# Low halves of q in zero-padded tiles of 128 rows for the score products of a hybrid decoder trunk

## The chip, the cores and the metric

The kernel runs on one core of a Trainium2 chip. The metric is the device time of one execution in microseconds. The engines are named PE (TensorE, the matrix products), DVE (VectorE), ACT (ScalarE), POOL (GpSimd) and SP (SyncE, which issues DMAs here). PEld is PE's weight load: a product on PE holds one operand (lhsT) in its array and streams the other (rhs) past it.

## The reference, cut to what matters

Two layers, each a half-step feed-forward network, a token mixer with four branches (A short convolution, B long convolution, C differential attention, D forgetting attention), and another feed-forward network. T = 512 tokens, model width 1024, fp32. The change touches the scores of C and D:

```python
# C: 4 heads x 2 maps of 64 channels, values of 128 channels
logits = jnp.einsum('bqhmd,bkhmd->bmhqk', q[:, q0:q1], k[:, :q1]) * scale + bias   # bias: -slope * distance
p = jax.nn.softmax(logits, axis=-1)
pd = p[:, 0] - lam * p[:, 1]
outs.append(jnp.einsum('bhqk,bkhd->bqhd', pd, v[:, :q1]))
...
# D: 8 heads of 64 channels
logits = jnp.einsum('bqhd,bkhd->bhqk', q[:, q0:q1], k[:, :q1]) * scale + bias      # bias: cumulative log forget gate, causal
p = jax.nn.softmax(logits, axis=-1)
outs.append(jnp.einsum('bhqk,bkhd->bqhd', p, v[:, :q1]))
```

Queries go in blocks of 128, so block i sees the keys 0 to 128 (i + 1).

## The kernel before

**Exact halves.** Every fp32 operand is a sum of a rounded high half and a low half, both in a format that PE multiplies at full rate (F32R). A product of two operands is made of high x high, high x low and low x high. For the projections and the feed-forward networks `mm3` (L127 to L131) issues the three: L129 is w_hi x_hi, L130 w_hi x_lo, L131 w_lo x_hi, with weight blocks of 128x128 as lhsT and 512 columns of x as rhs. The weights stream from memory in chunks of 8 blocks; `load` issues the DMA on SP, ACT casts the high half (L99), DVE subtracts the low half (L100).

**Queries and keys.** `q_of` and `k_of` each run one projection of 24 products for two maps of 64 channels: map 0 in partitions 0 to 63, map 1 in 64 to 127 (the slices `LANES`). `q_of` scales q by -1/8 on DVE (L476); ACT writes each map's high halves to both halves of the partitions of a tile of its own (`qh`, two tiles), and DVE writes the low halves of both maps into one tile `ql`, each map in its own 64 partitions. `k_of` puts the high halves of a map in its own 64 partitions and the low halves in the other 64. A score then takes two products: L501 with all 128 rows (q_hi against k_hi and against k_lo at once), and L502 with the 64 rows of the map's lanes (q_lo against k_hi):

```python
PE.matmul(out=p[:, :n], lhsT=q[0][m][:, c], rhs=k[m][:, :n], start=True, stop=False)
PE.matmul(out=p[:, :n], lhsT=q[1][r, c], rhs=k[m][r, :n], start=False, stop=not masked)
```

The columns n are 256, 256, 384 and 512 for the query blocks 0 to 3 (at least 256). In D a third product in bf16 (L504, 128 columns) adds the causal mask; in C the mask lies in the bias tile.

**What follows a score.** DVE adds the bias and takes the row's extreme (L519), ACT takes the exponential with its sum (L521). In C, `combine` (L597 to L600) forms p0 - lambda p1 of a row block on DVE; in D, `scale_rows` divides by the sum (L704, L705). `transposed` (L531) turns the row blocks by ten 128x128 transposes on PE, ACT and DVE make high and low halves of them (`ph` L150, `pl` L143), and `weigh` (L547) multiplies by the values.

**The order of work.** PE takes its products in the order in which the code emits them. For one C head that is: scores of query blocks 0 and 1 (eight products of 256 columns), the q projection of the next head, scores of blocks 2 and 3 (four of 384 and four of 512), the k projection, the output products of branch A (`merge`, 12), the ten transposes, a gate projection, weigh, another merge, sums over partitions, a gate, and the spread of a row of norms (L187). For one of the eight sets of D (a pair of heads x 2 maps) it is: the scores of four blocks with their masks, the q or k projection of the next pair (for the last pair a gate), the transposes, a gate, weigh, a merge. DVE's and ACT's work is set by the same code: `late` holds low halves and other second steps, which `settle` issues behind the next group of products, and `spare` holds the taps of B's long convolution (L383), which `cover` takes one at a time behind groups in C. In C, DVE keeps the order of the code (`manual_schedule`). The combination of the last row block (`combine(NQ - 1)`) is queued in `late` and comes behind the products of the k projection.

**Places.** Work tiles of 128x512 take places from the pool `sp` (65 of them), taken over by a new tile when the old one's last reader is done. Permanent tiles lie in the pool `cp`. PSUM has 8 places.

Of the kernel before, what the change touches and what calls it, by code (L numbers as in the profile page):

```python
# [15 lines left out]
P = 128  # L16
# [10 lines left out]
# column offsets of w_in  # L27
# [9 lines left out]
# chunks of weights that are loaded and split ahead of their use  # L37
AHEAD = 3
# taps of the long convolution that go with a group of products: in A and B, in C, in D
PACE = (3, 1, 5)  # L40
# steps of a boundary's second half in front of the first half's sums and of its spread norms
# [14 lines left out]
def build(tc, ws, xT, vecs, wdf, lamv, fb, consts, outT):  # L56
    """Emits the program; returns the order in which it takes the 128 x 128 blocks of the weights from ws."""
    nc = tc.nc
    order = []
    with ExitStack() as ctx:  # L60
        cp = ctx.enter_context(tc.tile_pool(name="cp", bufs=1))
        sp = ctx.enter_context(tc.tile_pool(name="sp", bufs=65))
# [22 lines left out]
        # the stream of weight blocks  # L85
# [4 lines left out]
        def load(c, parts=1):  # L90
            """the hi and lo halves of chunk c of the stream"""
# [23 lines left out]
        # work that later groups of products are to cover  # L115
# [11 lines left out]
        def mm3(out, w, x, first, last):  # L127
            """out += w.T @ x with both operands in exact halves."""
            PE.matmul(out=out, lhsT=w[0], rhs=x[0], start=first, stop=False)  # L129
            PE.matmul(out=out, lhsT=w[0], rhs=x[1], start=False, stop=False)  # L130
            PE.matmul(out=out, lhsT=w[1], rhs=x[0], start=False, stop=last)  # L131
# [22 lines left out]
        def split(src, scale=None, s="x"):  # L154
            """hi and lo halves of a tile, optionally times a scale first; the lo halves come with the next group."""
# [5 lines left out]
        def colsum(col, acc, c):  # L161
            """per-token sums over the partitions of acc[:, c], as columns."""
# [4 lines left out]
        def rstd(col, width, factor=1.0):  # L167
            """factor * (sums / width + eps) ** -0.5"""
# [7 lines left out]
        def diagonals(r):  # L176
            """a per-token column set on the diagonals of squares"""
# [6 lines left out]
        def spread(out, dg, n):  # L184
            """the diagonals of n squares as a row, the same in all partitions."""
# [4 lines left out]
        def rows_of(acc, width):  # L190
            """rstd of the sums over acc's partitions; the diagonals come with the next group."""
# [7 lines left out]
        def square_into(acc, src):  # L199
            """acc + src ** 2; acc None: src ** 2"""  # L200
# [7 lines left out]
        def boundary(post, pre, first):  # L208
            """h += factor * rms_norm(y) * g with y = products of post, then g * h of the next stage in halves,
            its first six groups of products and the per-token rstd as columns and as rows.  # L210

            The last tile of y and the first groups go by halves of the tokens, so that one half's norms are
            covered by the other half's products."""
            xs = []

            def new_x(k, c):
                """hi now, lo as a closure"""
# [8 lines left out]
            def outer(k, c):  # L226
                """products of row block k for the first four groups and the tokens c"""
# [17 lines left out]
            else:  # L245
# [10 lines left out]
                def last(a, b, h):  # L256
                    """steps a to b of the trailing tiles' products for the token half h"""
# [78 lines left out]
        # ---- feed-forward  # L336
# [29 lines left out]
        # ---- token mixing  # L366
# [6 lines left out]
        def mixer(l, entry):  # L373
# [13 lines left out]
            # lambda, on all partitions  # L387
# [15 lines left out]
            # B: gated linear unit and long convolution  # L403
# [22 lines left out]
            # A: short convolution  # L426
# [16 lines left out]
            def values(c0):  # L443
                """by tokens: [token, 512 channels] for each block of 128 tokens"""
# [15 lines left out]
            def paired(p, scale):  # L460
                """64-channel heads' halves side by side, for 128 output partitions: [hi lo] of even, [lo hi] of odd"""
# [11 lines left out]
            def q_of(c0):  # L473
                """-q/8 of two 64-channel maps: each map's hi halves on both halves of the partitions; lo halves"""
                q = slot()
                V.scalar_tensor_tensor(out=q, in0=proj(c0), scalar=-0.125, in1=rb, op0=ALU.mult, op1=ALU.mult)  # L476
                hi, lo = [slot(F32R, "qh"), slot(F32R, "qh")], slot(F32R, "ql")
# [4 lines left out]
                late.extend(lambda m=m: lo_of(lo[LANES[m]], q[LANES[m]], hi[m][LANES[m]]) for m in range(2))  # L482
# [348 lines left out]
```

## Time and profile before

| what | value |
|---|---|
| median of 3 runs | 2768.29 us (2768.15 to 2768.41) |
| span of the profiled execution, first to last instruction | 2767.0 us |
| mean granted TensorE clock | 0.998 |
| PE busy | 2748.0 us, 99% of the span, 13196 instructions |
| PEld busy | 2288.5 us, 83% |
| DVE busy | 1617.2 us, 58% |
| ACT busy | 1014.9 us, 37% |
| POOL busy | 57.0 us, 2% |
| HBM read, over the span | 250.48 MB, 91 GB/s |

The profiled execution has no time of its own beside its span; the span is 1.3 us under the median of the runs. Products on PE are pipelined, so the durations of neighbouring products overlap, and the distance from one start to the next tells how long PE needs for one. PEld rows are weight loads; a load that lies under the product before it costs nothing. The share of busy time is an average over stages. Which wait ends last in the attention stages is read from the timeline of these stages.

### The profile page before, as it was taken

Reading aid. Unit: us, or ns where it says so; the run is one execution under the profiler, and the core shown is the slowest. Engines: PE = TensorE matmul, PEld = TensorE weight load, DVE = VectorE, ACT = ScalarE, POOL = GpSimd, SP = SyncE. Lnnn points to the kernel's source line nnn. Section 1 sums busy time; section 2 is a strip of 40 time slices with the busy share of each in tenths; the row PEclk is TensorE's granted clock in tenths of the full one; section 3 lists DMA queues with packets and bytes.
Section 4 is the critical chain, followed back from the end, with each engine's and each line's share of the span. In section 5 each row is a group of like instructions: output and inputs, shape, how many; then the busy total and the mean of one; then the engine's idle time right before and its main releaser. Section 6 shows DMA issues by size and latency. Waiting matters only on the chain.

```text
span 2767.0 us, 33140 instructions
## 1 busy us (share of the span) xinstructions
PE 2748.0 (99%) x13196; PEld 2288.5 (83%) x13196; DVE 1617.2 (58%) x2699; ACT 1014.9 (37%) x1569; POOL 57.0 (2%) x84
## 2 busy tenths in 40 slices
PE   9999999999999999999999999999999999999998
PEld 7888898878778898888888888988777788988887
DVE  6444269878686555442364432798777765554423
ACT  4322242444553343332342222424445533433221
POOL 0000000001000000000000000000010000000000
PEclk9999999999999999999999999999999999999999
DMA  4332222222222223233233322232222223222331
GB/s 169 99 99 95 96 94 93 84 69 77 88 77 96 92 84 106 92 99 99 84 99 99 97 94 99 86 99 78 68 84 84 81 88 99 92 95 96 99 99 54
DMA packets 73787, 254.75 MB, mean 92 GB/s; under 512 B 8465, under 2 KB 10897, under 8 KB 73633
## 3 DMA queue, kind: packets, MB, share of 16 engines
q1 hardware_dynamic: 69264, 246.45, 27.4%
q10 hardware_dynamic: 4368, 6.20, 0.8%
q8 instruction: 103, 1.69, 0.2%
q14 instruction: 52, 0.42, 0.1%
HBM read 250.48 MB, written 2.13 MB: 91 GB/s over the span
## 4 chain that ended last, share of the span: by engine, by line
PE 99%; DVE 0%; DMA 0%; ACT 0%; POOLq 0%; issue 0%; DVEq 0%; ACTq 0%
PE p L129 27%; PE p L131 27%; PE p L130 27%; PE pf L130 2%; PE pf L129 2%; PE pf L131 2%; PE sc L502 2%; PE o L547 1%; PE pl L129 1%; PE pl L131 1%; PE pl L130 1%; PE sc L501 1%; PE pv L454 1%; PE pv L453 1%; PE pv L455 1%; PE pt L531 1%
## 5 line engine op out<-in xcount | busy, mean ns | idle before, releaser
L99 ACT CAST wh<-raw 128x1024 fp32r<-128x1024 f32 (+1 forms) x465 | 488.4, 1051 | 1303.5 <-PE p L130 865.4
L129 PE MATMUL p<-xh,wh 128*128 128x512 f32 x2304 | 904.9, 393 | 0.0
L131 PE MATMUL p<-xh,wl 128*128 128x512 f32 x2304 | 897.4, 389 | 0.0
L130 PE MATMUL p<-xl,wh 128*128 128x512 f32 x2304 | 897.0, 389 | 0.0
L100 DVE TENSOR_TENSOR wl<-raw,wh 128x1024 fp32r<-128x1024 f32 (+1 forms) x465 | 566.7, 1219 | 396.2 <-ACT wh L99 395.3
L129 PEld LDWEIGHTS p<-xh,wh 128*128 128x128 f32 x2304 | 432.8, 188 | 90.8 <-issue 2.0
L131 PEld LDWEIGHTS p<-xh,wl 128*128 128x128 f32 x2304 | 432.4, 188 | 91.0
L130 PEld LDWEIGHTS p<-xl,wh 128*128 128x128 f32 x2304 | 432.7, 188 | 88.3 <-issue 0.5
L129 PE MATMUL p<-gh,wh 128*128 128x512 f32 x616 | 239.6, 389 | 0.0
L130 PE MATMUL p<-gl,wh 128*128 128x512 f32 x616 | 239.6, 389 | 0.0
L131 PE MATMUL p<-gh,wl 128*128 128x512 f32 x616 | 239.6, 389 | 0.0
L352 DVE TENSOR_TENSOR s<-p,rb 128x512 f32<-128x512 f32 x80 | 55.2, 691 | 238.8 <-PE p L131 238.8
L383 DVE SCALAR_TENSOR_TENSOR yc<-ba,vec,yc 128x489 f32<-128x489 f32 (+18 forms) x240 | 171.6, 728 | 1.8
L346 DVE TENSOR_TENSOR s<-p,rb 128x512 f32<-128x512 f32 x80 | 55.2, 690 | 153.4 <-PE p L131 153.3
L129 PEld LDWEIGHTS p<-gh,wh 128*128 128x128 f32 x616 | 115.6, 188 | 24.1
L130 PEld LDWEIGHTS p<-gl,wh 128*128 128x128 f32 x616 | 115.6, 188 | 24.1
L131 PEld LDWEIGHTS p<-gh,wl 128*128 128x128 f32 x616 | 115.6, 188 | 23.9
L129 PE MATMUL pf<-xh,wh 128*128 128x256 f32 (+1 forms) x352 | 104.5, 297 | 6.9 <-ACT wh L99 6.9
L130 PE MATMUL pf<-xl,wh 128*128 128x256 f32 (+1 forms) x352 | 104.4, 297 | 0.0
L131 PE MATMUL pf<-xh,wl 128*128 128x256 f32 (+1 forms) x352 | 104.0, 295 | 0.0
L521 ACT ACTIVATE e<-e,mx 128x128 f32<-128x128 f32 (+3 forms) x128 | 71.2, 557 | 49.4 <-DVE mx L519 39.1
L557 DVE TENSOR_TENSOR s<-p,rb 128x512 f32<-128x512 f32 x64 | 44.1, 688 | 64.5 <-PE p L131 64.5
(205 smaller groups left out, 3245.5 us busy)
## 6 DMA issues: line engine op xcount, KB each, us to landing
raw<-ws SPq DMA_DIRECT2D x463, 512.0 KB, 3.3
cb<-cum ACTq DMA_DIRECT2D x16, 256.0 KB, 3.4
h<-xT SPq DMA_DIRECT2D x8, 256.0 KB, 5.2
outT<-h SPq DMA_DIRECT2D x8, 128.0 KB, 1.7
outT<-h ACTq DMA_DIRECT2D x8, 128.0 KB, 1.7
raw<-ws SPq DMA_DIRECT2D x2, 256.0 KB, 4.7
cst<-consts ACTq DMA_DIRECT2D x1, 384.0 KB
s<-lamv ACTq DMA_DIRECT2D x2, 128.0 KB, 2.0
```

Of the source, the lines that this page charges most:

```text
L99: S.copy(out=wh[:, j], in_=raw[:, j])
L100: V.tensor_sub(out=wl[:, j], in0=raw[:, j], in1=wh[:, j].bitcast(F32))
L129: PE.matmul(out=out, lhsT=w[0], rhs=x[0], start=first, stop=False)
L130: PE.matmul(out=out, lhsT=w[0], rhs=x[1], start=False, stop=False)
L131: PE.matmul(out=out, lhsT=w[1], rhs=x[0], start=False, stop=last)
L346: V.tensor_mul(out=x, in0=pg, in1=rb)
L352: V.tensor_mul(out=u, in0=pu, in1=rb)
L383: V.scalar_tensor_tensor(out=acc[:, s:], in0=y[:, :T - s], scalar=vcol(wname, l, i * 4 + j), in1=acc[:, s:], op0=ALU.mult, op1=ALU.add)
L453: PE.matmul(out=pv[t], lhsT=xh, rhs=wh, start=k == 0, stop=False)
L502: PE.matmul(out=p[:, :n], lhsT=q[1][r, c], rhs=k[m][r, :n], start=False, stop=not masked)
L521: S.activation(out=e, in_=e, func=AF.Exp, scale=-1.0, bias=mx, accum_out=sums)
L557: V.tensor_mul(out=g, in0=p, in1=rb)
```

## The change

The low halves of q no longer come from the work pool. Four permanent tiles `qlo`, two pairs of one tile for each map, are set to zero once, at the start, in the 64 partitions of the other map. `q_of` takes the pairs in turn (`nq` counts) and writes each map's low half into the map's own 64 partitions. `scores` then multiplies whole tiles: 128 rows of `qlo` against 128 rows of k, where the zero rows meet the low halves of k. The work pool goes from 65 to 62 places. Comments and docstrings are blanked too, and line numbers behind the head of `q_of` grow by 1 to 5.

```diff
-        sp = ctx.enter_context(tc.tile_pool(name="sp", bufs=65))
+        sp = ctx.enter_context(tc.tile_pool(name="sp", bufs=62))
...
             def q_of(c0):
                 q = slot()
                 V.scalar_tensor_tensor(out=q, in0=proj(c0), scalar=-0.125, in1=rb, op0=ALU.mult, op1=ALU.mult)
-                hi, lo = [slot(F32R, "qh"), slot(F32R, "qh")], slot(F32R, "ql")
+                hi, lo = [slot(F32R, "qh"), slot(F32R, "qh")], qlo[nq[0] % 2]
+                nq[0] += 1
...
-                late.extend(lambda m=m: lo_of(lo[LANES[m]], q[LANES[m]], hi[m][LANES[m]]) for m in range(2))
+                late.extend(lambda m=m: lo_of(lo[m][LANES[m]], q[LANES[m]], hi[m][LANES[m]]) for m in range(2))
...
             def scores(q, k, m, i, masked):
                 p = ps("sc")
                 n = max(2, i + 1) * P
-                r = LANES[m]
                 c = slice(i * P, (i + 1) * P)
                 PE.matmul(out=p[:, :n], lhsT=q[0][m][:, c], rhs=k[m][:, :n], start=True, stop=False)
-                PE.matmul(out=p[:, :n], lhsT=q[1][r, c], rhs=k[m][r, :n], start=False, stop=not masked)
+                PE.matmul(out=p[:, :n], lhsT=q[1][m][:, c], rhs=k[m][:, :n], start=False, stop=not masked)
...
+        qlo, nq = [[cp.tile([P, T], F32R, name=f"qlo{i}{m}") for m in range(2)] for i in range(2)], [0]
+        for pair in qlo:
+            for m in range(2):
+                V.memset(pair[m][LANES[1 - m]].bitcast(F32), 0.0)
```

On PE, at the end of the first score stage of the first C head in layer 0 (`sc` is a score's place in PSUM, `k` and `qh` are the key and query tiles, `p` is the next projection), the program before has

```order
2430 L502 MATMUL sc_3905<-k_3810,ql_3768 128x256
2431 L501 MATMUL sc_3911<-k_3809,qh_3766 128x256
2432 L502 MATMUL sc_3911<-k_3809,ql_3768 128x256
2433 L501 MATMUL sc_3917<-k_3810,qh_3767 128x256
2434 L502 MATMUL sc_3917<-k_3810,ql_3768 128x256
2435 L129 MATMUL p_3928<-xh_2542,wh_3776 128x512
```

and the changed program, at the same place on PE, has

```order
2430 L503 MATMUL sc_3912<-k_3817,qlo_100 128x256
2431 L502 MATMUL sc_3918<-k_3816,qh_3774 128x256
2432 L503 MATMUL sc_3918<-k_3816,qlo_99 128x256
2433 L502 MATMUL sc_3924<-k_3817,qh_3775 128x256
2434 L503 MATMUL sc_3924<-k_3817,qlo_100 128x256
2435 L129 MATMUL p_3935<-xh_2550,wh_3783 128x512
```

The sequence is the same; the low-half products read a tile of each map's own instead of one shared tile.

On PE, at the transposes of the last C head in layer 0 (`e` are the tiles of the row blocks: the one with the highest number holds rows 0 and 2, the next row 1, the lowest row 3, the last; `pt` are the places of the four key blocks), the program before has

```order
2983 L531 MATMUL pt_5083<-cst,e_4899 128x128
2984 L531 MATMUL pt_5083<-cst,e_4898 128x128
2985 L531 MATMUL pt_5083<-cst,e_4899 128x128
2986 L531 MATMUL pt_5083<-cst,e_4897 128x128
2987 L531 MATMUL pt_5090<-cst,e_4898 128x128
2988 L531 MATMUL pt_5090<-cst,e_4899 128x128
2989 L531 MATMUL pt_5090<-cst,e_4897 128x128
2990 L531 MATMUL pt_5096<-cst,e_4899 128x128
2991 L531 MATMUL pt_5096<-cst,e_4897 128x128
2992 L531 MATMUL pt_5101<-cst,e_4897 128x128
```

and the changed program, at the same transposes on PE, has

```order
2983 L532 MATMUL pt_5086<-cst,e_4903 128x128
2984 L532 MATMUL pt_5086<-cst,e_4902 128x128
2985 L532 MATMUL pt_5086<-cst,e_4903 128x128
2986 L532 MATMUL pt_5093<-cst,e_4902 128x128
2987 L532 MATMUL pt_5093<-cst,e_4903 128x128
2988 L532 MATMUL pt_5099<-cst,e_4903 128x128
2989 L532 MATMUL pt_5086<-cst,e_4901 128x128
2990 L532 MATMUL pt_5093<-cst,e_4901 128x128
2991 L532 MATMUL pt_5099<-cst,e_4901 128x128
2992 L532 MATMUL pt_5104<-cst,e_4901 128x128
```

The four transposes that read the last row (e_4897 before, e_4901 after) stood fourth, seventh, ninth and tenth; now they are the last four.

On DVE, in the first set of D in layer 0 (`s` is the q projection scaled, `sums` and `e` the last row's sums and weights, `wl` a weight chunk's low half, `pl` the low halves of the transposed weights), the program before has

```order
726 L476 SCALAR_TENSOR_TENSOR s_5477<-p_5478,rb_2996 128x512
727 L704 RECIPROCAL sums_5442<-sums_5442 128x1
728 L705 TENSOR_SCALAR e_5436<-e_5436,sums_5442 128x512
729 L100 TENSOR_TENSOR wl_5608<-raw_5606,wh_5607 128x1024
730 L143 TENSOR_TENSOR pl_5528<-pt_5532,ph_5524 128x512
731 L143 TENSOR_TENSOR pl_5530<-pt_5539,ph_5526 128x384
732 L143 TENSOR_TENSOR pl_5529<-pt_5545,ph_5525 128x256
733 L143 TENSOR_TENSOR pl_5529<-pt_5550,ph_5525 128x128
734 L143 TENSOR_TENSOR ql_5519<-s_5477,qh_5517 64x512
735 L143 TENSOR_TENSOR ql_5519<-s_5477,qh_5518 64x512
```

and the changed program, in the same set on DVE, has

```order
730 L477 SCALAR_TENSOR_TENSOR s_5480<-p_5481,rb_3004 128x512
731 L705 RECIPROCAL sums_5445<-sums_5445 128x1
732 L706 TENSOR_SCALAR e_5439<-e_5439,sums_5445 128x512
733 L100 TENSOR_TENSOR wl_5610<-raw_5608,wh_5609 128x1024
734 L143 TENSOR_TENSOR qlo_101<-s_5480,qh_5520 64x512
735 L143 TENSOR_TENSOR qlo_102<-s_5480,qh_5521 64x512
736 L143 TENSOR_TENSOR pl_5530<-pt_5534,ph_5526 128x512
737 L143 TENSOR_TENSOR pl_5532<-pt_5541,ph_5528 128x384
738 L143 TENSOR_TENSOR pl_5531<-pt_5547,ph_5527 128x256
739 L143 TENSOR_TENSOR pl_5531<-pt_5552,ph_5527 128x128
```

The two low halves of q stood behind the four of the transposed weights; now they stand ahead of them.

## Rows read from the trace of the kernel before

**Rows 1.** The page's first part (busy time of each engine, share of the span, instructions) and the first line of its fourth part (shares of the chain that ended last, by engine).

```profile
PE 2748.0 (99%) x13196; PEld 2288.5 (83%) x13196; DVE 1617.2 (58%) x2699; ACT 1014.9 (37%) x1569; POOL 57.0 (2%) x84
...
PE 99%; DVE 0%; DMA 0%; ACT 0%; POOLq 0%; issue 0%; DVEq 0%; ACTq 0%
```

**Rows 2.** Timeline of PE and PEld at the first score stage of C head 0, layer 0: start in us, duration in us, engine, line and operation, what goes out and in, and the idle time before with its releaser.

```profile
528.04 0.39 PE L129 MATMUL p<-xh,wh 128*128 128x512 f32 x1
528.04 0.19 PEld L130 LDWEIGHTS p<-xl,wh 128*128 128x128 f32 x1
528.27 0.39 PE L130 MATMUL p<-xl,wh 128*128 128x512 f32 x1
...
528.72 0.28 PE L501 MATMUL sc<-k,qh 128*128 128x256 f32 x1
...
528.93 0.18 PEld L502 LDWEIGHTS sc<-k,ql 64*128 64x128 f32 x1 [0.24 <-issue]
528.93 0.38 PE L502 MATMUL sc<-k,ql 64*128 64x256 f32 x1
529.24 0.19 PEld L501 LDWEIGHTS sc<-k,qh 128*128 128x128 f32 x1
529.24 0.38 PE L501 MATMUL sc<-k,qh 128*128 128x256 f32 x1
...
531.45 0.39 PE L130 MATMUL p<-xl,wh 128*128 128x512 f32 x1
```

**Rows 3.** PE's timeline at the second score stage of the same head, with the second product of the k projection behind it.

```profile
536.69 0.33 PE L501 MATMUL sc<-k,qh 128*128 128x384 f32 x1
...
537.69 0.44 PE L502 MATMUL sc<-k,ql 64*128 64x384 f32 x1
538.05 0.50 PE L501 MATMUL sc<-k,qh 128*128 128x512 f32 x1
538.49 0.50 PE L502 MATMUL sc<-k,ql 64*128 64x512 f32 x1
...
540.11 0.39 PE L130 MATMUL p<-xl,wh 128*128 128x512 f32 x1
```

**Rows 4.** PE's timeline in the weigh stage of D's set 1, layer 0.

```profile
722.17 0.33 PE L547 MATMUL o<-ph,v 128*128 128x384 f32 x1
722.35 0.34 PE L547 MATMUL o<-pl,v 128*128 128x384 f32 x1
722.52 0.28 PE L547 MATMUL o<-ph,v 128*128 128x256 f32 x1
722.64 0.28 PE L547 MATMUL o<-pl,v 128*128 128x256 f32 x1
```

**Rows 5.** PE's timeline in the score stage of D's set 2, layer 0: its first product, its last mask product, and the first two products of the projection behind it.

```profile
725.74 0.28 PE L501 MATMUL sc<-k,qh 128*128 128x256 f32 x1
...
728.55 0.23 PE L504 MATMUL sc<-maskb,identb 128*128 128x128 bf16 x1
728.59 0.47 PE L129 MATMUL p<-xh,wh 128*128 128x512 f32 x1
728.90 0.39 PE L130 MATMUL p<-xl,wh 128*128 128x512 f32 x1
```

**Rows 6.** DVE's timeline in C head 1, layer 0, around the chain from the q projection to the last row's combination, and PE's transposes behind it.

```profile
572.38 0.72 DVE L383 SCALAR_TENSOR_TENSOR yc<-ba,vec,yc 128x485 f32<-128x485 f32 x1
574.81 0.69 DVE L476 SCALAR_TENSOR_TENSOR s<-p,rb 128x512 f32<-128x512 f32 x1 [1.71 <-PE p L131]
...
584.31 0.75 DVE L600 SCALAR_TENSOR_TENSOR e<-e,sums,e 128x512 f32<-128x512 f32 x1
...
585.99 1.25 PE L531 MATMUL pt<-cst,e 128*128 128x128 f32 x10
```

**Rows 7.** Timeline of ACT, DVE and PE in the last C head, layer 0 (windows of one engine each).

```profile
652.33 1.88 ACT L150 CAST qh<-s 64x512 fp32r<-64x512 f32 x3 [0.30 <-PE sc L501]
...
660.60 0.75 DVE L600 SCALAR_TENSOR_TENSOR e<-e,sums,e 128x512 f32<-128x512 f32 x1
...
661.81 1.25 PE L531 MATMUL pt<-cst,e 128*128 128x128 f32 x10
```

**Rows 8.** Timeline of ACT and DVE in D's set 1, layer 0: the high and low halves of the four transposed key blocks.

```profile
717.55 1.37 ACT L150 CAST ph<-pt 128x512 fp32r<-128x512 f32 x4
...
718.15 1.73 DVE L143 TENSOR_TENSOR pl<-pt,ph 128x512 fp32r<-128x512 f32 x4 [1.33 <-ACT ph L150]
```

**Rows 9.** Timeline of DVE and PE in the same set: the q projection's product with rb, the low halves of q, and the four transposes that read the last row.

```profile
714.41 0.69 DVE L476 SCALAR_TENSOR_TENSOR s<-p,rb 128x512 f32<-128x512 f32 x1 [0.97 <-PE p L131]
...
719.80 1.38 DVE L143 TENSOR_TENSOR ql<-s,qh 64x512 fp32r<-64x512 f32 x2
...
715.74 0.66 PE L531 MATMUL pt<-cst,e 128*128 128x128 f32 x4 [0.72 <-DVE e L705]
```

**Rows 10.** Timeline of DVE and PE in D's set 7, layer 0.

```profile
830.99 0.48 DVE L705 TENSOR_SCALAR e<-e,sums 128x512 f32<-128x512 f32 x1
...
831.77 1.25 PE L531 MATMUL pt<-cst,e 128*128 128x128 f32 x10
```

**Rows 11.** DVE's timeline at the start of the program.

```profile
1.13 0.22 DVE L766 MEMSET zeros<- 128x192 f32 x1
...
4.44 0.21 DVE L401 TENSOR_SCALAR subg<-vec 128x1 f32<-128x1 f32 x2 [3.09 <-DMA vec<-vecs]
```

## Prediction

> **What bounds the kernel now.** I read the page's first part, then the chain that ended last, then TensorE's (PE's) timeline in the stages that the change touches. The page gives PE 99% of a span of 2767.0 us, and the chain is 99% PE as well [rows 1]: the kernel ends when PE's list of 13196 products ends, and the other engines matter only where PE waits for them. So the question is how long PE's score products take, and whether the engine that feeds its transposes can follow a faster PE.
>
> The timeline of a score stage answers the first half [rows 2]. Ahead of it, in a projection, products of 512 columns start 0.23 us apart (528.04, 528.27), and each weight load (PEld, 0.19 us) starts together with the product before it, so it is covered. In the score stage that is no longer so. The load for the low-half product (L502, 64 rows) starts at 528.93, in the same instant as its product, while the full product ahead of it had started at 528.72. The next full load starts at 529.24, again together with its own product. So each change between 128 and 64 rows leaves a load standing in the open. Products of 256 columns then take 0.31 us from start to start (528.93 to 529.24), those of 384 take 0.36 (537.69 to 538.05) and those of 512 take 0.44 [rows 2, 3]. The weigh stage has products of the same widths with 128 rows on both sides: 384 columns take 0.17 from start to start, 256 take 0.12 [rows 4]. The difference is 0.19 at both widths, and 0.21 for 512 columns against the projection's 0.23: the length of a load. That is what the change goes for.
>
> **The change part by part.** *Score products of C.* A head has two score stages. The first, with eight products of 256 columns, runs from its first product to the second product of the projection behind it (the first one there still pays for the load) in 531.45 - 528.72 = 2.73 us [rows 2]. At the covered rate it is 8 x 0.12 + 0.23 = 1.19: 1.54 saved. The second stage (four of 384, four of 512) takes 540.11 - 536.69 = 3.42 [rows 3]; covered it is 4 x 0.17 + 4 x 0.23 + 0.23, with unrounded pitches 1.82: 1.60 saved. The program has 8 heads (two layers of four): 8 x 3.14 = 25.1 us.
>
> *Score products of D.* A set has two score products for each of four query blocks, and a bf16 product of 128 columns that adds the mask. From the first one to the second projection product it takes 728.90 - 725.74 = 3.16 us [rows 5]. Covered, the f32 products are 4 x 0.12 + 2 x 0.17 + 2 x 0.23 + 0.23 = 1.50. The masks stay as they are. The row behind the last mask shows what one costs: the product after it starts 0.04 later, and that product takes 0.31 to the next start (728.59 to 728.90) instead of 0.23 [rows 5]. That is 0.13 for a mask with what it uncovers, and 4 x 0.13 = 0.53 for a set. So a set goes to 2.03 and saves 1.13; 16 sets: 18.1 us. From below, if the product behind a mask is held only by its load, a set saves 1.22, 1.4 us more in all; from above, if the masks keep the whole load in the open on both sides, see the third rival. I take 0.13, since it stands in the row for the same pair of operations.
>
> Gross: 25.1 + 18.1 = **43.2 us**.
>
> *What is given back in waits.* In C VectorE (DVE) has a fixed chain from the q projection (L476) over the exponentials' first halves, a weight chunk, the q low halves and the last row's combination (L597 to L600). In head 1 it starts at 574.81 and ends with L600 at 584.31 + 0.75 = 585.06, 10.25 us, nearly without a gap [rows 6]. PE's ten transposes start at 585.99 and the fourth of them, about 0.3 later, is the first that reads that row: 1.25 us of margin. The first score stage's saving lies ahead of L476, and DVE is idle 1.71 before it [rows 6], so that saving passes through. The second stage's 1.60 lies beside the chain: it eats the margin and leaves PE about 0.4 of waiting. Three heads in each layer: 2.3 us. In the fourth head the row ends at 660.60 + 0.75 = 661.35 and the transposes start at 661.81 [rows 7]. The new order puts the six that don't read row 3 first, some 0.6 us of the ten's 1.25 [rows 7], which makes the margin 1.06 and the wait some 0.6. In that head ScalarE also waits for a place (0.30 on a score product, [rows 7]). By the built order a q product there gets a place that scores still read, and a weight low half gets one that the weigh stage is still reading; I put 0.4 us on PE for that, between 0 and one evacuation of 0.43 (1.73 / 4, [rows 8]). Fourth heads: 2 x 1.0 = 2.0 us.
>
> In D the margins are wider except in two sets. In set 1 PE already waits 0.72 for DVE's last row (L705) behind L476 at 714.41, and DVE was idle only 0.97 before L476 [rows 9]: of 1.13 about 0.16 is lost. In set 7 L705 ends at 830.99 + 0.48 = 831.47, DVE is busy throughout, and the transposes start at 831.77 with the first reader of that row 0.6 later by the same order [rows 10]: margin near 0.96, lost about 0.2. Two layers: 0.7 us. In all 2.3 + 2.0 + 0.7 = **5.0 us** go back.
>
> *The rest.* Four memsets of 64 x 512 at the start: a memset of 128 x 192 takes 0.22 [rows 11], so by columns each is some 0.5 to 0.6, 2.4 at most, and DVE stands idle 3.09 there for the vectors' DMA [rows 11]: nothing on the path. Without that cover they would cost 2.4. The low halves cost DVE the same two instructions; in D their 1.38 us at 719.80 move ahead of the weights' four low halves at 718.15 [rows 8, 9]. Those would end up to 1.4 later, at about 721.3, against weigh, whose products of 384 columns start at 722.17 [rows 4]; and DVE waits 1.33 for ScalarE ahead of them, which the moved work can fill [rows 8]. So I count nothing. Three places fewer in the pool lengthen some waits; beyond those two of the fourth head I found none in PE's waits of the built program.
>
> Sum: 43.2 - 5.0 = 38.2 off the profiled span of 2767.0 gives 2728.8. The runs' median, 2768.29, is 1.3 above that span, which I keep: **2730 us**.
>
> A rule speaks against all of this. The projection's rows show loads of 0.19 us that start with the product before them though both use all 128 rows [rows 2]. The Trainium skill, page "TensorE: Matmul & The Clock Gate", Part 3, section "The mechanism", says in its list of what overlaps that weight loads overlap with running products only when their row groups differ. By that rule alone full-row loads would stay in the open, and the sum would be 0 saved in place of 43.2. The trace doesn't agree: L129 to L131 start every 0.23 us with loads of 0.19 between [rows 2]; what the rows show in the open is the change of rows.
>
> **The rivals.** *DVE sets the pace of C (faster, but less).* If DVE's work ahead of L476 doesn't move up with PE, each C head keeps only its margin of 1.25: 8 x 1.25 = 10.0, with D's 18.1 - 0.7 = 17.4 it is 27.4 in all: 2741 us. For: DVE has hardly a gap in the chain. Against: its 1.71 idle before L476. Chance 0.10.
>
> *Nothing is given back (faster, more).* The waits are hidden and the product behind a mask is held only by its load: 43.2 + 1.4 gives 2724 us. For: ScalarE's queue moves up too, and DVE's short gaps could close. Against: the 10.25 us chain. Chance 0.08.
>
> *The masks keep the drain.* A mask has bf16 weights between f32 ones; if with full rows it leaves a load open on each side, 64 x 2 x 0.19 = 24 us are not saved: 2754 us. Against: 0.04 between mask and next product [rows 5]. Chance 0.03.
>
> *The change doesn't do what it says.* If the open loads belong not to the change of rows but to the score products as such (their stationary q tiles come from other tiles than a projection's), nothing changes: 2768 us. This is also where the rule above would end. Against: weigh alternates its operands in the same way at 0.12 and 0.17 [rows 4]. Chance 0.04.
>
> *Slower: evacuations in series with weigh.* With 62 places, the high and low halves of the transposed weights (1.37 + 1.73 = 3.10 us a set, [rows 8]) may have to wait for places whose last reader is a product just ahead on PE. If they came in series in all 24 heads and sets, 24 x 3.1 = 74 us would be added to 2730: 2804 us. It decides from 38.2 / 24 = 1.6 us a set. For: the pool is what shrinks, and one such place exists in each layer. Against: it is one. Chance 0.03.
>
> **How the numbers follow.** Forecast 0.72, rivals in order 0.10, 0.08, 0.03, 0.04, 0.03. The range takes the forecast with the unknown costs (0 to 5 given back, masks at either bound), the second rival at the low end and the first at the high end: 2723 to 2742, which leaves out 0.10. A measurement tells 0.2% (5.5 us) from no change. Faster: 0.72 + 0.10 + 0.08 + 0.03 = 0.93; same 0.04; slower 0.03.
>
> **What the profile after would show.** Score products of 256, 384 and 512 columns at starts 0.12, 0.17 and 0.23 apart, each load under the product before; C's first stage 1.2 to 1.3 us, its second 1.8, a D set 2.0. Waits of PE for DVE's last row of 0.3 to 0.7 at the transposes of each C head. Wrong if 0.31 stays between products of 256 columns, if a mask leaves over 0.2 open, or if PE waits over 1 us at the transposes or inside weigh of many heads.

## The result and the profile after

The changed kernel takes **2730.58 us** (median of 4 runs, 2729.99 to 2731.29) against 2768.22 for the kernel before (4 runs). The ratio is 0.9864, 95% interval 0.985 to 0.9878: 1.36% less, 37.6 us. The profiled execution has a span of 2728.8 us at a granted clock of 0.999. All times are medians; one execution of e10 below took 3096.32 us at a granted clock of 0.821, and without it that run's median is 2725.50 in place of 2725.65.

The page after, first part and the shares of the chain by engine [rows 1]:

```profile
PE 2706.4 (99%) x13196; PEld 2280.8 (84%) x13196; DVE 1617.6 (59%) x2703; ACT 1016.6 (37%) x1569; POOL 55.5 (2%) x84
...
PE 96%; DVE 3%; ACT 1%; issue 0%; DMA 0%; POOLq 0%; DVEq 0%; ACTq 0%
```

PE has the same 13196 products and is busy 41.6 us less; the chain that ended last, which was 99% PE, now runs 4% through DVE and ACT. Both halves of the story are in these two lines: cheaper products, and new waits. (The 4% are work of DVE and ACT that stands in the chain; PE's waiting itself is about 6 us, as the timelines show.)

The timeline of PE and PEld at the first score stage of C head 0, layer 0 [rows 2]:

```profile
528.47 0.28 PE L502 MATMUL sc<-k,qh 128*128 128x256 f32 x1
528.47 0.19 PEld L503 LDWEIGHTS sc<-k,qlo 128*128 128x128 f32 x1
528.58 0.28 PE L503 MATMUL sc<-k,qlo 128*128 128x256 f32 x1
528.58 0.19 PEld L502 LDWEIGHTS sc<-k,qh 128*128 128x128 f32 x1
...
529.41 0.40 PE L129 MATMUL p<-xh,wh 128*128 128x512 f32 x1
529.64 0.39 PE L130 MATMUL p<-xl,wh 128*128 128x512 f32 x1
```

Each load now starts with the product before its own, as in a projection, and products of 256 columns start 0.12 apart instead of 0.31. The stage takes 529.64 - 528.47 = 1.17 us (before 2.73). The second stage of that head [rows 3] and the score stage of D's set 2 [rows 5], PE's timeline:

```profile
534.86 0.34 PE L502 MATMUL sc<-k,qh 128*128 128x384 f32 x1
...
536.71 0.39 PE L130 MATMUL p<-xl,wh 128*128 128x512 f32 x1
...
714.24 0.28 PE L502 MATMUL sc<-k,qh 128*128 128x256 f32 x1
...
715.90 0.23 PE L505 MATMUL sc<-maskb,identb 128*128 128x128 bf16 x1
715.94 0.48 PE L129 MATMUL p<-xh,wh 128*128 128x512 f32 x1
716.26 0.40 PE L130 MATMUL p<-xl,wh 128*128 128x512 f32 x1
```

They take 1.85 (before 3.42) and 2.02 (before 3.16). The mask still costs 0.04 and leaves its neighbour at 0.32 instead of 0.23. Over the program: 8 x (1.56 + 1.57) + 16 x 1.14 = 43.3 us saved in the score stages.

What came back stands at the transposes. DVE and PE in C head 1 [rows 6], the windows of one engine each:

```profile
570.25 0.69 DVE L477 SCALAR_TENSOR_TENSOR s<-p,rb 128x512 f32<-128x512 f32 x1
...
579.75 0.75 DVE L601 SCALAR_TENSOR_TENSOR e<-e,sums,e 128x512 f32<-128x512 f32 x1
...
579.84 0.49 PE L532 MATMUL pt<-cst,e 128*128 128x128 f32 x3
580.56 0.98 PE L532 MATMUL pt<-cst,e 128*128 128x128 f32 x7 [0.24 <-DVE e L601]
```

DVE's idle time of 1.71 us before the q product is gone, its chain still takes 580.50 - 570.25 = 10.25 us, and PE's fourth transpose has to wait for its end. In all the ten take 0.45 us longer than before: three take 0.33, and the fourth comes 0.72 after the first.

The last C head [rows 7], DVE and PE:

```profile
641.58 0.69 DVE L477 SCALAR_TENSOR_TENSOR s<-p,rb 128x512 f32<-128x512 f32 x1 [1.04 <-PE sc L502]
...
651.09 0.75 DVE L601 SCALAR_TENSOR_TENSOR e<-e,sums,e 128x512 f32<-128x512 f32 x1
...
658.60 1.09 DVE L143 TENSOR_TENSOR pl<-pt,ph 128x384 fp32r<-128x384 f32 x3 [0.97 <-PE o L548]
...
650.24 0.81 PE L532 MATMUL pt<-cst,e 128*128 128x128 f32 x6
651.90 0.66 PE L532 MATMUL pt<-cst,e 128*128 128x128 f32 x4 [0.85 <-DVE e L601]
...
658.56 0.33 PE L548 MATMUL o<-ph,vh 128*128 128x384 f32 x1
658.73 0.39 PE L129 MATMUL p<-yah,wh 128*128 128x512 f32 x1
658.96 0.40 PE L130 MATMUL p<-yal,wh 128*128 128x512 f32 x1
659.21 0.44 PE L548 MATMUL o<-pl,vh 128*128 128x384 f32 x1
```

Here the q product waits 1.04 us on DVE for a *score product* of PE: a place that scores still read. PE loses 1.06 at the transposes. Inside weigh the low half for the second key block waits 0.97 on DVE for a place that weigh's own products read; but in the order of the changed program two products of the next merge stand in that gap (658.73, 658.96), and PE loses only some 0.12 there.

The memsets at the start [rows 11] and D's set 1 [rows 8, 9], DVE:

```profile
1.49 2.37 DVE L771 MEMSET qlo<- 64x512 f32 x4
...
4.40 0.21 DVE L401 TENSOR_SCALAR subg<-vec 128x1 f32<-128x1 f32 x2 [0.53 <-DMA vec<-vecs]
...
705.24 1.40 DVE L143 TENSOR_TENSOR qlo<-s,qh 64x512 fp32r<-64x512 f32 x2
706.82 1.73 DVE L143 TENSOR_TENSOR pl<-pt,ph 128x512 fp32r<-128x512 f32 x4 [0.18 <-ACT ph L150]
```

The memsets fill DVE's wait for the vectors' DMA. In D the low halves of q fill what had been a wait of 1.33 us for ACT, of which 0.18 is left.

### The profile page after: what moved, and what is told of

Its sections match the earlier page's. It is cut to its first block, busy times and chain, and to the rows that moved or that the text cites. A ratio compares the mean times of both kernels' runs of the same rounds, so it can differ in the third digit from the quotient of the medians.

```text
span 2728.8 us, 33159 instructions
## 1 busy us (share of the span) xinstructions
PE 2706.4 (99%) x13196; PEld 2280.8 (84%) x13196; DVE 1617.6 (59%) x2703; ACT 1016.6 (37%) x1569; POOL 55.5 (2%) x84
## 4 chain that ended last, share of the span: by engine, by line
PE 96%; DVE 3%; ACT 1%; issue 0%; DMA 0%; POOLq 0%; DVEq 0%; ACTq 0%
PE p L129 26%; PE p L130 26%; PE p L131 26%; PE pf L130 2%; PE pf L129 2%; PE pf L131 2%; PE o L548 1%; PE pl L129 1%; PE pl L131 1%; PE pl L130 1%; PE pv L454 1%; PE pv L455 1%; PE pv L453 1%; PE pt L532 1%; PE st L187 1%; PE sc L502 1%
## 5 line engine op out<-in xcount | busy, mean ns | idle before, releaser
L129 PE MATMUL p<-xh,wh 128*128 128x512 f32 x2304 | 903.3, 392 | 0.0
L129 PEld LDWEIGHTS p<-xh,wh 128*128 128x128 f32 x2304 | 432.8, 188 | 88.0 <-PE pt L532 0.5
L129 PE MATMUL p<-gh,wh 128*128 128x512 f32 x616 | 239.6, 389 | 0.0
L129 PEld LDWEIGHTS p<-gh,wh 128*128 128x128 f32 x616 | 115.6, 188 | 24.0
L129 PE MATMUL pf<-xh,wh 128*128 128x256 f32 (+1 forms) x352 | 104.5, 297 | 6.8 <-ACT wh L99 6.8
L522 ACT ACTIVATE e<-e,mx 128x128 f32<-128x128 f32 (+3 forms) x128 | 71.2, 557 | 53.8 <-DVE mx L520 42.6
```

The source lines that it names most:

```text
L522: S.activation(out=e, in_=e, func=AF.Exp, scale=-1.0, bias=mx, accum_out=sums)
```

## The experiments

The two theories under test: **(1)** what the change removes is the weight load that stands in the open at each change between 128 and 64 rows; **(2)** what is given back comes from DVE's chain ahead of C's last row block, and in the last heads also from places of the pool. The rivals are that part of the gain belongs to the new tiles rather than to the rows, that 64-row products are slow as such, and that the smaller pool is harmless or the whole of the cost.

| run | median us | ratio to before (95%) |
|---|---|---|
| changed kernel | 2730.58 | 0.9864 (0.985 to 0.9878) |
| e1_rows64 | 2767.61 | 0.9998 (0.9988 to 1.0007) |
| e2_rows64_d | 2747.55 | 0.9925 (0.9911 to 0.994) |
| e3_rows64_c | 2750.80 | 0.9937 (0.992 to 0.9953) |
| e4_comb_first | 2727.40 | 0.9852 (0.9837 to 0.9867) |
| e5_halves_same, e6_halves_alternate | 2731.65, 2731.81 | one run each |
| e7_no_mask | 2725.13 | 0.9845 (0.9831 to 0.986) |
| e8_pool62 | 2777.49 | 1.0035 (1.0022 to 1.0047) |
| e9_three_tiles | 2729.77 | 0.986 (0.9846 to 0.9873) |
| e10_three_tiles_comb | 2725.65 | 0.9845 (0.9832 to 0.9858) |
| e11_d_equal_lanes | 2736.22 | one run |
| e12_masks_last | 2727.69 | 0.9852 (0.9837 to 0.9867) |

**Rows alone, by branch (e1, e2, e3).** The low-half product reads 64 rows again, in both branches, in D alone, in C alone:

```diff
-PE.matmul(out=p[:, :n], lhsT=q[1][m][:, c], rhs=k[m][:, :n], ...)
+PE.matmul(out=p[:, :n], lhsT=q[1][m][LANES[m], c], rhs=k[m][LANES[m], :n], ...)
```

> The changed kernel with one thing put back: the low-half products of C and D read only the 64 rows of the map's lanes again, out of the same zero-padded tiles. Tiles, memsets, 62 places and the order stay as in the changed kernel. Theory (a weight load is left open at every change of rows): the score stages go back to 2.73, 2.82, 3.42 and 3.16 us, 43.3 us in all, and the waits at the transposes that the faster stages brought (5.6 us, with 0.2 in weigh) go away: 2768 us, within 1.5. Rival (part of the gain comes from the tiles of their own, for instance from the order of the low halves on DVE, or the pool of 62 costs something by itself): the score stages keep part of the gain, or the time is off 2768 by more than 2 us.

> The changed kernel with 64-row low-half products in D alone; C keeps 128 rows. Theory: C saves 25.2 us in its score stages and gives back 2.7 at the transposes of its first three heads and 2.4 in the last ones, so the time is 2768.2 - 20 = 2748 us. Rival (DVE sets the pace of C, and the gain sits in D): above 2755 us.

> The changed kernel with 64-row low-half products in C alone; D keeps 128 rows. Theory: D saves 16 x 1.15 = 18.3 us less 0.75 of waits in its set 7, so 2768.2 - 17.6 = 2750.6 us, and the two savings (this and the one of C alone) add to the whole, 37.6, within 1. Rival (the stages hand waits to each other): the sum is off by over 2 us.

With 64 rows everywhere the time is back at 2767.6, all of the gain gone, although tiles, memsets, order and 62 places are those of the changed kernel: the gain is the rows'. (The waits did not all go, as had been expected: the transposes of each last C head still take 0.24 us longer than in the kernel before.) The two branches save 20.7 and 17.4 us (from 2768.25), together 38.1 against 37.6 for both. DVE does not set C's pace: C alone is at 2747.55, not above 2755.

**What a 64-row product costs, and what a change of rows costs (e5, e6, e11).** C's first stage (e5, e6) or D's whole stage (e11) gets its full products first and its 64-row low halves after them:

```diff
-F(0,0) H(0,0) F(0,1) H(0,1) F(1,0) H(1,0) F(1,1) H(1,1)     # C; (block, map); F 128 rows, H 64 rows
+F(0,0) F(0,1) F(1,0) F(1,1) H(0,0) H(1,0) H(0,1) H(1,1)     # e5: map 0's lanes twice, then map 1's
+F(0,0) F(0,1) F(1,0) F(1,1) H(0,0) H(0,1) H(1,0) H(1,1)     # e6: lanes alternate
-F0 H0 mask0 F1 H1 mask1 F2 H2 mask2 F3 H3 mask3              # D, one map
+F0 F1 F2 F3 H0 H1 H2 H3 mask0 mask1 mask2 mask3              # e11
```

> The changed kernel with another order in C's first score stage alone: the four 128-row products of blocks 0 and 1 first, then the four low-half products with 64 rows again, the two of map 0 (lanes 0 to 63) and then the two of map 1 (lanes 64 to 127). The rest of the kernel keeps 128 rows. This splits what the 64-row product costs from what a change costs. Theory (a change of rows leaves the load open): starts 0.12 apart inside the four full products and inside each pair of equal lanes, and 0.31 at each of the three changes (full to lanes 0-63, lanes 0-63 to 64-127, 64-127 to full). Rival A (a 64-row load never runs ahead of its product): 0.31 at all of the four 64-row products. Rival B (the open load comes from rows that overlap; disjoint lanes are free): 0.31 on the way in and out, but 0.12 or less from lanes 0-63 to lanes 64-127.

> As the run with equal lanes side by side, but the four low-half products alternate between the lanes (0-63, 64-127, 0-63, 64-127). Theory (any change of rows leaves the load open): 0.31 from each low-half product to the next. Rival A (64-row loads never run ahead): 0.31 as well, so this run alone doesn't part the two; the run with equal lanes does. Rival B (disjoint lanes are free): 0.12 or less between them, and 0.31 only on the way in and out.

> The changed kernel with D's products of a set in another order and 64-row low halves there: the four 128-row products, then the four low-half products of the set's one map (all in the same 64 lanes), then the four masks. C keeps 128 rows. The run with pairs of equal lanes could not be read, since products of both lane halves ran side by side; here only one half is in use. Theory (a load is left open where the running product's rows overlap its own without being the same): 0.19 open once, from the last full product to the first low half, then starts 0.12, 0.12 and 0.17 apart inside the low halves. Rival (a 64-row load is never covered by a product in its own rows): 0.31, 0.31 and 0.36 inside the low halves.

PE's timeline of e6, the stage and the projection behind it (x4 is a run of four products; its time is from the first start to the last end):

```profile
527.96 0.63 PE L616 MATMUL sc<-k,qh 128*128 128x256 f32 x4
528.52 0.50 PE L620 MATMUL sc<-k,qlo 64*128 64x256 f32 x4
528.95 0.50 PE L129 MATMUL p<-xh,wh 128*128 128x512 f32 x1
529.29 0.39 PE L130 MATMUL p<-xl,wh 128*128 128x512 f32 x1
```

A narrower window, from 528.91 on, holds the last two of the four low halves alone:

```profile
528.74 0.28 PE L620 MATMUL sc<-k,qlo 64*128 64x256 f32 x2
```

The four low halves take 0.43 us to the next start, less than the 4 x 0.12 = 0.48 of four covered products one after the other, although the way out still shows an open load (0.34 instead of 0.23 for L129) and the way in as well (four full products take 0.56 instead of 0.47). And the last two together take 0.28 us from start to end, as long as one product of 256 columns takes alone. So products in different lanes lay side by side. e5 shows nearly the same, 0.44 (528.93 to 529.37), so its order did not tell equal lanes from different ones, and the theory that *any* change of rows opens a load is wrong: between the two lane halves nothing is left open. The Trainium skill, page "TensorE: Matmul & The Clock Gate", Part 3, section "The mechanism", shows row tiles of different row groups running at once; the 0.43 us agrees.

Equal lanes alone stand in e11, PE's timeline of D's set 2:

```profile
713.42 0.81 PE L713 MATMUL sc<-k,qh 128*128 128x256 f32 x4
714.16 0.90 PE L715 MATMUL sc<-k,qlo 64*128 64x256 f32 x4
714.99 0.40 PE L717 MATMUL sc<-maskb,identb 128*128 128x128 bf16 x4
...
715.51 0.39 PE L130 MATMUL p<-xl,wh 128*128 128x512 f32 x1
```

Narrower windows start at the second, the third and the fourth low half:

```profile
714.38 0.45 PE L715 MATMUL sc<-k,qlo 64*128 64x256 f32 x2
714.50 0.56 PE L715 MATMUL sc<-k,qlo 64*128 64x384 f32 x2
714.67 0.39 PE L715 MATMUL sc<-k,qlo 64*128 64x512 f32 x1
```

Four low halves (256, 256, 384 and 512 columns) in the same 64 lanes take 714.99 - 714.16 = 0.83 us: 0.64 covered plus 0.19, and not the 1.42 that 0.31, 0.31, 0.36 and 0.44 would make. The single starts are 0.22, 0.12 and 0.17 apart, where 0.12, 0.12 and 0.17 had been expected. The second and the third are covered pitches; the 0.22 holds about half of the open load from 128 to 64 rows (the other 0.1 lies ahead of the first low half), and the remaining 0.09 stands between the last low half and the first mask. A 64-row load is covered by a product in its own rows. What stays open is the load between 128 and 64 rows, in either direction. The run takes 5.6 us more than the changed kernel. The score stages, 715.51 - 713.42 = 2.09 in place of 2.02, make 1.3 of it; PE waits 2.1 and 1.9 longer for DVE at the transposes of set 7 in the two layers; and behind the second of these waits the granted clock stands near 0.50 from 2174 to 2177 us, which costs 1.6. About 0.8 comes back ahead of the first score, where executions differ. The list of what overlaps in that section of the Trainium skill, by which loads overlap only where row groups differ, does not agree with this run, nor with the projections; the text ahead of that list also names a background weight buffer, and no run here tells which way a covered load takes.

**The waits (e4).** One move on DVE in C:

```diff
-late.append(lambda: combine(NQ - 1))
+late.insert(0, lambda: combine(NQ - 1))
```

> The changed kernel, with one move on DVE: in C the combination of the last row block is queued ahead of the low halves of q, which nobody needs before the next head's scores, instead of behind them. Theory (PE waits at C's transposes because that row stands 1.4 us late at the end of DVE's chain): the waits of 0.45 in the first three heads and of 1.06 in the last ones go, 4.8 us in all: 2725.7 us. Rival (the last heads' waits come from places of the smaller pool, a q tile that ScalarE can't write yet): only the 2.7 us of the first three heads go: 2727.8 us, and the transposes of the last heads still show over 0.8 of waiting. Second rival (ScalarE's exponential of row 3 is late as well): under 2 us are gained.

2727.40: 3.2 us, neither the 4.8 nor the rival's 2.7 by its own reasons. The transposes give back 4.85 between them, in the first three heads 0.45 each and in the last 1.06 each: the theory holds there. But 0.76 us is lost in each last head's weigh (its products and the merge behind them take 5.55 us, in the changed kernel 4.79), as DVE's and PE's timelines of e4 show:

```profile
640.22 0.69 DVE L477 SCALAR_TENSOR_TENSOR s<-p,rb 128x512 f32<-128x512 f32 x1 [1.04 <-PE sc L502]
...
655.43 0.39 PE L548 MATMUL o<-ph,vh 128*128 128x512 f32 x1
656.33 0.50 PE L548 MATMUL o<-pl,vh 128*128 128x512 f32 x1 [0.51 <-DVE pl L143]
```

DVE still stands 1.04 us for the place of the q product, and all that follows it on DVE is late by that much. The last row is now out of that chain's way; the low halves of the transposed weights, further down, are not, and PE meets them 0.51 too early. The wait moved on.

**The pool (e8, e9, e10).** e8 is the kernel before with `bufs=62` and nothing else; e9 is the changed kernel with three tiles and 63 places; e10 is e9 with the move of e4:

```diff
-qlo = [[a0, b0], [a1, b1]], bufs=62
+qlo = [[a, b0], [a, b1]], bufs=63
```

> The kernel before with a pool of 62 places instead of 65 and nothing else. Theory (the pool costs nothing of weight as long as the score stages are slow): 2768.2 to 2769.5 us, with at most some 0.5 us of waiting more in the last C heads. Rival (three places fewer put the high and low halves of the transposed weights in series with weigh): 2772 us or more.

> The changed kernel with three zero-padded tiles instead of four (both pairs share the tile of map 0, whose scores are done before its next low half is written) and with the room spent on a place more in the pool, 63. Theory (the last C heads' wait inside weigh, 0.34 us less 0.22 that comes back right behind it, is a place that is taken over too early): with one place more it goes, 2730.2 to 2730.6 us less at most 0.7, so 2729.9 to 2730.5, and the trace shows weigh at its full rate of 1.93 us there. Rival (63 places hand the same place over): weigh keeps 2.26 us.

> Three tiles and 63 places as in the run before, and the combination of the last row block ahead of the low halves of q. Theory: with 62 places that move won 4.85 us at C's transposes and lost 1.6 inside weigh of the last heads, where the second product waited for a low half whose place was still read; with one place more the 1.6 stay won: 2725.3 to 2726 us. Rival (63 don't do either): 2727.4 us as with 62.

e8 missed: it is 9.7 us slower than the kernel before measured with it (2767.81), where at most 1.3 was expected. All of it lies in the two last C heads. DVE and PE there in layer 0, then busy times, granted clock (0.50, third from the end) and DMA of a stretch behind the wait:

```profile
651.75 0.42 DVE L519 CUSTOM_DVE_ANT_0 e<-sc,bias 128x256 f32<-128x256 f32 x1 [6.64 <-PE sc L501]
...
661.23 0.82 PE L531 MATMUL pt<-cst,e 128*128 128x128 f32 x6
665.25 0.66 PE L531 MATMUL pt<-cst,e 128*128 128x128 f32 x4 [3.20 <-DVE e L600]
...
666.82 0.63 PE L129 MATMUL p<-xh,wh 128*128 128x512 f32 x1
667.24 0.63 PE L130 MATMUL p<-xl,wh 128*128 128x512 f32 x1
...
666.10:669.30 3.20, 3.20 (x9) 2.50 (x8) 3.10 (x5) 2.27 (x5) 0.00 (x0) 0.50 0.21 47
```

DVE's exponential step for block 1 waits 6.64 us for a place that PE's scores of the later blocks still read, and PE then waits 3.20 at the transposes, which take 3.42 us longer than in the kernel before. The wait costs more than itself: 0.7 us after its end the granted clock falls from 1.00 to 0.50, the lower of its two levels (1.2 in place of 2.4 GHz), for some 3.4 us, and products of 512 columns start 0.43 apart instead of 0.23. That is another 1.76 us, so a last head loses 5.2. The changed kernel does not meet this because its low halves of q have left the pool: three places were given up, and some of the need for them as well. e1 shows it: it has 62 places and 64-row low halves like e8, but keeps the low halves out of the pool, and takes 2767.61.

e9 takes 2729.77, just under what was expected. The last head's transposes lose 0.67 instead of 1.06 us and weigh runs at its full rate (1.93 us, as in the kernel before), so one place is worth 0.4 there besides weigh's wait. e10 keeps what e4 won, DVE and PE in the last head:

```profile
639.33 0.69 DVE L477 SCALAR_TENSOR_TENSOR s<-p,rb 128x512 f32<-128x512 f32 x1
...
647.57 0.75 DVE L601 SCALAR_TENSOR_TENSOR e<-e,sums,e 128x512 f32<-128x512 f32 x1
...
648.91 1.25 PE L532 MATMUL pt<-cst,e 128*128 128x128 f32 x10
655.47 0.39 PE L548 MATMUL o<-ph,vh 128*128 128x512 f32 x1
655.70 0.40 PE L548 MATMUL o<-pl,vh 128*128 128x512 f32 x1
```

The q product no longer waits for a place, and the ten transposes and weigh run without a gap: 2725.65 us, as expected, 4.9 below the changed kernel and 42.6 below the one before, the fastest version that does all of the work.

**The masks (e7, e12).** e7 leaves D's mask product out; e12 is e10 with a set's four masks behind its eight products.

> The changed kernel without D's bf16 mask product (so D's queries see the later keys of their own block too: that part of the computation is left out). It prices the mask with full rows. Theory (0.04 for the mask itself and 0.09 for the load it leaves open behind it): a D set's score stage goes from 2.01 to 1.49 us, 16 x 0.52 = 8.4 us less, less up to 1 us of new waits for DVE: 2722 to 2723.5 us. Rival (the mask costs only its own 0.04): 2728 us.

> The run with three tiles and the early combination, with D's four masks of a set behind all eight score products instead of one behind each pair. Theory (a mask costs its own 0.04 and the 0.09 of the load behind it, because that load is longer than the mask's product): four masks in a row of equal weights leave the f32 load open only once, so a set saves 3 x 0.09 = 0.27 us less what the masks' own loads leave open, 16 sets up to 4.3 us, down to about 2722 us, less the waits of DVE, which gets its first scores of a set some 1.3 us later. Rival (DVE's delay reaches PE's transposes in most sets): slower than the run without this move.

In e7 a set takes 715.17 - 713.65 = 1.52 us instead of 2.02, so a mask costs 0.125, near the 0.13 of the sum: the rival that it costs only its own 0.04 falls. Of 16 x 0.50 = 8.0 us the kernel shows 5.45, or 5.0 when each run is taken against the kernel before that was measured with it (42.7 against 37.6), and so misses the 2722 to 2723.5 us. The rest came back as waits for DVE at the transposes, 2.95 us where at most 1 was expected, 1.95 of it in set 7 of the two layers. e12 takes the same price from the other side. Four masks in a row start 0.05 apart and a set takes 1.82 us, 0.20 less than 2.02 (3.2 us in all), yet the run is 2.0 slower than e10. PE's timeline in set 7:

```profile
809.90 0.49 PE L532 MATMUL pt<-cst,e 128*128 128x128 f32 x3
811.17 0.55 PE L532 MATMUL pt<-cst,e 128*128 128x128 f32 x3 [0.78 <-DVE e L706]
812.90 0.66 PE L532 MATMUL pt<-cst,e 128*128 128x128 f32 x4 [1.18 <-DVE e L706]
```

These ten take 2.4 us longer than an undisturbed set's, in either layer. In layer 1 of the profiled execution (2728.17 us, the longest of the four) the granted clock also stands near 0.50 from 2166 to 2169 us, right behind the same two waits, and PE loses 1.6 us more; in layer 0 it stays at 1.00 behind them. DVE has no idle time in that set, and in e12 a weight chunk also came to stand ahead of the last exponential; which of the two weighs more was not separated. The rival was right on the sign and wrong on "most sets": it is one set a layer.

## Why the prediction was right, point by point

*The bound.* PE was the bound, and the open load was the reason for the slow score products: e1 gives all of it back with the rows alone. The reason as the prediction put it, "each change between 128 and 64 rows", is what e11 and e6 leave standing; "any change of rows", as it was put for e1 and e5, is not.

*The gross gain* was forecast at 43.2 us and measured 43.3: C's stages at 1.17 and 1.85 against 1.19 and 1.82, a D set at 2.02 against 2.03. The mask at 0.13, taken from the one row pair behind a set's last mask, held at every mask, and e7 measured it at 0.125. How it splits is less sure: four masks in a row start 0.05 apart, so the rest, about 0.07, comes with the loads around a mask, where the prediction had 0.04 and 0.09.

*What was given back* was forecast at 5.0 and measured at about 5.9, distributed differently. The first three heads lost 0.45 each, forecast 0.4. The last heads lost 1.06 at the transposes and a net 0.12 by weigh, forecast 0.6 and 0.4: the total was near (1.2 against 1.0), but the parts were not. The place that scores still read delays DVE's whole chain and so the transposes, where the prediction had one estimate of 0.4 for both places, and the 1.06 lies outside the 0.3 to 0.7 that it gave for the transposes of each head; e9 shows 0.4 of the 1.06 going with one place more, and e4 all of it going with the order of DVE. In weigh two merge products that PE takes meanwhile hide most of the gap. D's set 1 lost nothing, forecast 0.16: DVE's wait for the DMA of `cb`, further up in its chain, shrank from 0.86 to 0.61 us, room that the sum had not counted; set 7 lost 0.25 in one layer and 0.50 in the other, forecast 0.2.

*The rest.* The memsets took 2.37 us in an idle DVE, forecast 2.4 at most. The missing 0.8 between 43.3 - 5.9 and the 38.2 of the spans lies in small pieces, 0.25 ahead of the first score and 0.47 behind the last set of D, which differ from run to run. Most of the latter is the clock: the program's last four products on PE (L187) took 1.22 us at a granted clock of 0.50 in the kernel before, and 0.71 at 1.00 in the changed one, where the clock falls a little later. So it is luck that the span came out at the 2728.8 of the sum to the digit: the waits were 0.9 longer than forecast, and these pieces hid most of that. By the medians, 43.3 - 5.9 = 37.4 stands against a measured 37.6, and the forecast of 2730 was 0.6 too low.

*The rivals.* DVE as the pace of C falls with e2. "Nothing is given back" falls with the waits in the trace, though e10 shows that nearly all of C's part of them can be had. The masks do not keep a whole load of 0.19 open on either side: e7 prices one at 0.125 with everything around it. That the open loads belong to the score products as such falls with the 0.12 from start to start in the profile after, and with e1. The slow rival, places that put evacuations behind PE, was given one mechanism in the wrong place: e8 shows that the pool at 62 alone costs 9.7 us, not in 24 sets but in one head of each layer, at the transposes and not inside weigh, and e1 that it is the low halves' leaving the pool that kept the change clear of it. The prediction's "three places fewer" left out the places that the change gives back.

## What to carry to other kernels

Where products of different row counts alternate, look at the start of each weight load: if it coincides with its own product instead of the one before, a load is in the open at each change, and zero rows that make all products alike cost nothing on PE here (0.12 from start to start with 256 columns, as in weigh). When PE gets faster in a stage, work out for each stage which engine's chain starts before the saving and ends behind it; what it anchors is lost, and moving work that nobody needs soon out of that chain (here the low halves of q) gives it back, if no place that is still read holds the chain up (e4 against e10). A change of a pool's size should be weighed with the tiles that leave the pool, and tried by itself. When a wait of PE is priced, the granted clock behind it belongs to the price.

## What the runs showed of the hardware that was not expected

Four 64-row products in two lane halves took 0.43 us with 256 columns each, where four 128-row products take 0.47 and an open load comes on top: products in different halves of the rows ran side by side. Equal lanes in a row are covered like full rows (starts 0.12 and 0.17 apart at 256 and 384 columns in e11). Four bf16 mask products of equal weights in a row start 0.05 us apart, so more than half of the 0.125 that a mask costs between f32 products comes with the loads around it. And a wait of PE can cost half as much again as it lasts: behind the 3.20 us of e8 the granted clock stood at 0.50 for some 3.4 us in both layers, 1.76 us more each time.
